# Tokens by place in a chunk of four, and S5 preparation moved from GpSimd to VectorE and ScalarE, in a two-layer S5 and attention kernel

## The chip, the cores and the metric

The kernel runs on one core of one Trainium2 chip. The metric is the device time of one execution in microseconds. A core has TensorE (PE in the profile, its weight loads PEld), VectorE (DVE), ScalarE (ACT), GpSimd (POOL) and SyncE (SP), which issues most of the transfers.

## The reference: what is computed

Two layers of half a feed-forward block, a mixer and another half block over 256 tokens of width 1024, all in float32. Cut to what matters here:

```python
for l in range(DEPTH):                       # 2
    x = x + 0.5 * swiglu(rms_norm(x, norm_ffn1[l]), ffn1_wi[l], ffn1_wo[l])
    h = rms_norm(x, norm_mix[l])
    (u, q_raw, k_cmp, v_cmp, k_sel, v_sel, k_win, v_win,
     nsa_gate, gate_a, gate_b) = jnp.split(h @ w_in[l], SPLIT_POINTS, axis=-1)
    y_a = s5_branch(u, ...)                  # 32 groups of 16 channels, 64 complex states each
    y_b = nsa_branch(q_raw, k_cmp, ...) @ nsa_w_up[l]
    merged = sigmoid(gate_a) * y_a + sigmoid(gate_b) * y_b
    x = x + merged @ w_out[l]
    x = x + 0.5 * swiglu(rms_norm(x, norm_ffn2[l]), ffn2_wi[l], ffn2_wo[l])
```

`s5_branch` discretizes a diagonal complex system (abar, bbar from lambda, dt, b), runs st[t] = abar st[t-1] + bbar u[t] over the tokens, and gives gelu(Re(c st) + d u), which goes through a gated product. `nsa_branch` rotates and normalizes q and k, compresses blocks of 32 tokens of k and v (stride 16) by a two-layer product, and attends to compressed, selected and windowed keys.

## The kernel before

**Products.** The wide products run as three passes of a split float32: `_split0` (L157 on ScalarE, L158 on VectorE) and `split` (L337, both engines) make a high part and a low part of each weight chunk of 128x1024, and `mm3` issues whi·hh, whi·hl and wlo·hh (L369 to L371). Chunks come through four buffers each of raw, high and low parts, and are asked for by `k.next()`, two ahead. A feed-forward block goes through 11 pieces of 256 hidden columns, whose results are transposed (L484) and split again.

**Background.** What isn't a wide product is written as generators that are pulled at every `k.next()` until their declared costs reach a budget. In ffn1 the generator is `prep`: `s5_scalars`, `s5_tables`, `s5_mats`. They build, from the layer's S5 parameters, the matrices G (input, `r` tiles), K (within a chunk of four tokens) and C (output) by complex products (`cmul`, L580 to L591: four products and two sums), by selections of a group's rows (L803), by transposes (L811) and by copies into place (L530 in `gcopy`). With `M=G` the four products of a `cmul` go to GpSimd (L580, L582, L587, L589) and the two sums to VectorE (L584, L591).

**The mixer.** `mix` takes h through chunks of w_in: 512 columns for u, 384 for compressed keys and values, 408 for the others, 512 for q, then the gates. After the first it makes uT (L1274, L1275: transposes and copies), and `s5_main` becomes the background: sixteen copies of 32 partitions (L868 on ScalarE, L870 on VectorE) turn uT into U4, which has the token within a chunk of four and the channel on the partitions and the chunk along the row; two sets of products G·U4 (L538, banks ya and yb); a rotation by tables (`rotate`, L925 to L933), two scans of 128x1024 (L885), a rotation back into Sp; the output products K·U4 and C·Sp (L903, tiles of 32 columns, 64 moving columns); gelu, and the split that gives yT. Meanwhile `compress` multiplies weights by strided columns of kc2 (L538, 45 moving columns), its result goes through `normrope` (L992 to L1005, on GpSimd L344, L345, L1004), is copied to kb (L1096), and is transposed in `compress2` (L1103). `normrope_q` does the same for q (L1056 to L1066).

**Order.** A scheduler in the framework orders the instructions of each engine at build time; each engine then runs its own list in order and waits for semaphores where it must. So an instruction that waits holds up all that stand behind it on its engine. The output leaves on SP's queue (L381).

Of the kernel before, what the change touches and what calls it, by code (L numbers as in the profile page):

```python
# [34 lines left out]

def shape_constants():
    a = np.zeros((128, 128 + CONST_W), np.float32)
    a[:, :128] = np.eye(128)
# [14 lines left out]
    put('cos', c.reshape(2, 128, 64).transpose(1, 0, 2))  # L53
    put('sin', s.reshape(2, 128, 64).transpose(1, 0, 2))
# [20 lines left out]
class Model:  # L75
# [497 lines left out]

    def cmul(k, o, a, b, tmp, cost, M=None, conj=False):

        V = k.nc.vector
        M = M or V
        c = cost if M is V else 0.0
        t0, t1 = tmp(), tmp()
        M.tensor_mul(t0, a[0], b[0])  # L580
        yield c
        M.tensor_mul(t1, a[1], b[1])  # L582
        yield c
# [3 lines left out]
        M.tensor_mul(t2, a[0], b[1])  # L587
        yield c
        M.tensor_mul(t3, a[1], b[0])  # L589
        yield c  # L590
# [130 lines left out]
    def s5_tables(k):  # L721
# [9 lines left out]
        k.gcopy(de, P['m4'][:, :, None].to_broadcast([128, 16, 64]))  # L731
# [37 lines left out]
    def s5_mats(k):  # L769
# [87 lines left out]
    def s5_main(k, uT):  # L857
# [35 lines left out]
        yt = r4().rearrange("p (a t s) -> p a t s", a=4, s=4)  # L893

        T = ((P['K'], U4), (P['C'][0], Sp[0]), (P['C'][1], Sp[1]))
        for h in range(2):
            bk = k.bank((128, 2, 4, 64), 'yb')
            for i, (m, v) in enumerate(T):
                for a in range(2):
                    for s in range(4):  # L900
                        for q in range(4):
                            p = h * 8 + a * 4 + q
                            nc.tensor.matmul(bk[q * 32:(q + 1) * 32, a, s], m[:, p, s * 32:(s + 1) * 32], v[:, p],  # L903
# [519 lines left out]
```

## Time and profile before

| | us |
|---|---|
| median of 3 runs | 1187.76 (1186.48 to 1188.71) |
| the profiled execution | 1188.25 |
| its span, first to last instruction | 1186.4 |
| PE busy | 1161.3 (98%) |
| DVE busy | 839.6 (71%) |
| ACT busy | 674.6 (57%) |
| POOL busy | 231.8 (20%) |

The span is 1.85 us shorter than the execution's time. Busy times of PE count overlapping matmuls once; a matmul of 512 columns is listed at 0.39 us, but the next starts 0.23 us later, and the distance between starts is what it costs in a run of them. On VectorE, too, an instruction starts some 0.08 us before the listed end of the one ahead of it. The two layers repeat: what stands at 225 us in the first stands at some 815 in the second.

### The profile page before, as it was taken

How to read it: one execution, taken by the hardware profiler on the slowest of the kernel's cores; microseconds unless marked ns; L12 is line 12 of the kernel's file. 1: busy time of each engine (PE TensorE's matmuls, PEld its weight loads, DVE VectorE, ACT ScalarE, POOL GpSimd, SP SyncE). 2: the span in 40 equal slices, each digit the busy share in tenths (PEclk: the TensorE clock that was granted, in tenths of full speed). 3: DMA queues.
4: the chain of work that ended last, by engine and by line, in shares of the span. 5: the costliest groups of instructions: out<-in, count | busy, mean ns of one | idle time of the engine just before them, and what ended most of it. 6: DMA issues, size and time to landing. Idle time of an engine off the chain costs nothing. (4 is left out here: it accounts for less than half of the span.)

```text
span 1186.4 us, 18796 instructions
## 1 busy us (share of the span) xinstructions
PE 1161.3 (98%) x6724; PEld 944.9 (80%) x6724; DVE 839.6 (71%) x1494; ACT 674.6 (57%) x1176; POOL 231.8 (20%) x285
## 2 busy tenths in 40 slices
PE   9999999999999999999999999999999999999998
PEld 6888777887877888888888887778778778888886
DVE  5797979586875755555667987886878756655554
ACT  6655554745765565554566555546657646655552
POOL 3002654044032000000030043711341310000000
PEclk9999999999999999999999999999999999999999
DMA  8766555364443566565565656445635435665662
GB/s 237 226 194 184 170 154 179 105 192 144 145 140 104 165 211 187 185 190 183 187 188 178 195 162 182 142 152 155 199 107 173 129 107 160 214 185 188 188 185 89
DMA packets 150078, 200.48 MB, mean 169 GB/s; under 512 B 9952, under 2 KB 120832, under 8 KB 149984
## 3 DMA queue, kind: packets, MB, share of 16 engines
q1 hardware_dynamic: 148848, 197.46, 54.3%
q0 software_dynamic: 1136, 1.82, 0.9%
q8 instruction: 53, 0.87, 0.3%
q14 instruction: 41, 0.34, 0.1%
HBM read 198.18 MB, written 1.05 MB: 168 GB/s over the span
## 5 line engine op out<-in xcount | busy, mean ns | idle before, releaser
L158 DVE SCALAR_TENSOR_TENSOR wlo<-raw,gcol,whi 128x512 fp32r<-128x512 f32 (+2 forms) x480 | 359.0, 785 | 110.0 <-ACT whi L157 107.6
L157 ACT ACTIVATE whi<-raw,gcol 128x512 fp32r<-128x512 f32 (+2 forms) x480 | 316.1, 710 | 193.0 <-PE gu L370 92.4
L369 PE MATMUL gu<-whi,hh 128*128 128x512 f32 (+2 forms) x944 | 372.2, 394 | 0.6 <-ACT whi L157 0.6
L371 PE MATMUL gu<-wlo,hh 128*128 128x512 f32 (+2 forms) x944 | 369.1, 396 | 2.3 <-DVE wlo L158 2.3
L370 PE MATMUL gu<-whi,hl 128*128 128x512 f32 (+2 forms) x944 | 368.9, 391 | 0.0
L337 DVE TENSOR_TENSOR wlo<-raw,whi 128x1024 fp32r<-128x1024 f32 x128 | 160.9, 1259 | 103.1 <-ACT whi L337 101.1
L337 ACT CAST whi<-raw 128x1024 fp32r<-128x1024 f32 x128 | 134.5, 1053 | 135.4 <-PE gu L370 112.1
L371 PEld LDWEIGHTS gu<-wlo,hh 128*128 128x128 f32 x944 | 177.8, 189 | 37.8 <-DVE wlo L158 2.6
L370 PEld LDWEIGHTS gu<-whi,hl 128*128 128x128 f32 x944 | 178.2, 189 | 35.2
L369 PEld LDWEIGHTS gu<-whi,hh 128*128 128x128 f32 x944 | 178.3, 189 | 34.5 <-ACT whi L157 0.8
L344 POOL TENSOR_SCALAR rs<-ss 128x1 f32<-128x1 f32 (+3 forms) x22 | 7.2, 328 | 378.4 <-ACT w2k L351 351.6
L370 PE MATMUL yb<-whi,w1k 128*128 128x512 f32 x176 | 71.4, 406 | 0.7 <-DVE w1k L337 0.7
L371 PE MATMUL yb<-wlo,w1k 128*128 128x512 f32 x176 | 69.2, 393 | 0.0
L369 PE MATMUL yb<-whi,w1k 128*128 128x512 f32 x176 | 69.0, 395 | 0.0
L370 PE MATMUL ya<-whi,w1k 128*128 128x512 f32 x176 | 68.8, 391 | 0.0
L371 PE MATMUL ya<-wlo,w1k 128*128 128x512 f32 x176 | 68.7, 391 | 0.0
L369 PE MATMUL ya<-whi,w1k 128*128 128x512 f32 x176 | 68.2, 393 | 0.0
L1207 POOL TENSOR_SCALAR w2k<-w2k,sm 128x128 f32<-128x128 f32 (+1 forms) x64 | 38.9, 629 | 100.6 <-ACT w2k L1191 63.2
L337 ACT CAST w1k<-tr 128x256 fp32r<-128x256 f32 x88 | 32.5, 370 | 45.7 <-PE tr L484 45.7
L501 DVE SCALAR_TENSOR_TENSOR w1k<-gu,rs,w1k 128x256 f32<-128x256 f32 x88 | 42.0, 479 | 16.2 <-ACT w1k L500 16.2
L500 ACT ACTIVATE w1k<-gu,rs 128x256 f32<-128x256 f32 x88 | 40.9, 467 | 20.0 <-PE gu L371 13.7
L337 DVE TENSOR_TENSOR w1k<-tr,w1k 128x256 fp32r<-128x256 f32 x88 | 36.7, 418 | 10.1 <-ACT w1k L337 10.0
(316 smaller groups left out, 1502.1 us busy)
## 6 DMA issues: line engine op xcount, KB each, us to landing
raw<-in_ffn_wi_dram SPq DMA_DIRECT2D x352, 256.0 KB, 3.3
raw<-in_ffn_wo_dram SPq DMA_DIRECT2D x88, 512.0 KB, 3.6
raw<-in_w_in_dram SPq DMA_DIRECT2D x48, 512.0 KB, 4.5
raw<-in_ssm_w_glu_dram SPq DMA_DIRECT2D x32, 256.0 KB, 3.4
raw<-in_w_out_dram SPq DMA_DIRECT2D x16, 512.0 KB, 3.3
raw<-in_cmp_w_dram SPq DMA_DIRECT2D x8, 512.0 KB, 4.8
raw<-in_nsa_w_up_dram SPq DMA_DIRECT2D x16, 256.0 KB, 4.1
raw<-in_w_in_dram SPq DMA_DIRECT2D x8, 408.0 KB, 4.2
```

Of the source, the lines that this page charges most:

```text
L157: k.hi_ins[i] = k.nc.scalar.activation(hi[:, s], r[:, s], AF.Copy, scale=c)
L158: k.lo_ins = k.nc.vector.scalar_tensor_tensor(lo[:, s], r[:, s], c, hi[:, s].bitcast(F32), op0=ALU.mult, op1=ALU.subtract)
L337: return k.nc.scalar.copy(hi, src), k.nc.vector.tensor_sub(lo, src, hi.bitcast(F32))
L344: k.nc.gpsimd.tensor_scalar(a, ss, scale, EPS, op0=ALU.mult, op1=ALU.add)
L369: mm(ps, a[0], b[0], start=first, stop=False)
L370: mm(ps, a[1], b[0], start=False, stop=False)
L371: return mm(ps, a[0], b[1], start=False, stop=last)
L500: m = nc.scalar.activation(sg, ps[t][:, :256], AF.Silu, scale=r[t])
L501: nc.vector.scalar_tensor_tensor(a, ps[t][:, 256:], r[t], sg, op0=ALU.mult, op1=ALU.mult)
L1207: G.tensor_scalar(w[:, i], p[:, i], cf[:, j:j + 1], 0.0, op0=ALU.mult, op1=ALU.add)
```

## The change

Tokens are stored by place: token t of each 128 goes to partition 32·(t mod 4) + t div 4 (`PLACE`; x is permuted before the launch, the constant tables alike, and `store` writes each 128x512 of the output by four transfers of 32 rows, alternately from SP's queue and ScalarE's). With that order, U4 is a 32x32-block transpose of u, done by VectorE straight behind the scaling by ScalarE, so the PE transposes, their copies and the sixteen narrow copies are left out. The output products swap their operands: U4 and Sp are stationary (64 columns), K and C move (128 columns), 48 matmuls a layer instead of 192; the result is put through gelu, transposed by PE (eight per layer) and split. kc2 is laid out so that the compression reads 33 adjacent columns instead of 45 strided ones.

In the S5 preparation, all products of `cmul` are on VectorE; the four selections (128x1024 each) are halved between ScalarE and VectorE, the ten copies into `ks` likewise, and the copy into `de` goes to ScalarE. The products of `normrope` and `normrope_q` move from GpSimd to VectorE. The budget per chunk grows from 0.75 to 1.2, and the generator waits longer before its first step.

```diff
+PLACE = 4 * (np.arange(128) % 32) + np.arange(128) // 32
...
+    def store(k, t, h, xs):
+        for u in range(4):
+            o = bass.AP(tensor=k.out.tensor, offset=k.out.offset + (t * 128 + u) * D + h * 512,
+                        ap=[[4 * D, 32], [1, 512]])
+            (k.nc.sync if u % 2 else k.nc.scalar).dma_start(o, xs[u * 32:(u + 1) * 32])
...
-                    k.nc.sync.dma_start(k.out[0, t * 128:(t + 1) * 128, h * 512:(h + 1) * 512], xs)
+                    k.store(t, h, xs)
...
-    def cmul(k, o, a, b, tmp, cost, M=None, conj=False):
+    def cmul(k, o, a, b, tmp, cost, conj=False):
...
-        M.tensor_mul(t0, a[0], b[0])
-        yield c
+        V.tensor_mul(t0, a[0], b[0])
+        yield cost
...
-                G.tensor_scalar(xx[:, :, g], X[i].rearrange("p a t c -> p (a t) c"), k.C('m64')[:, g:g + 1], 0.0,
-                                op0=ALU.mult, op1=ALU.add)
+                o, v, w = xx[:, :, g], X[i].rearrange("p a t c -> p (a t) c"), k.C('m64')[:, g:g + 1]
+                if g:
+                    V.tensor_scalar(o, v, w, None, op0=ALU.mult)
+                else:
+                    S.activation(o, v, AF.Copy, scale=w)
+                yield 1.2
...
-                k.gcopy(ks[t * 32:(t + 1) * 32, :, s], lag[r * 32:(r + 1) * 32])
+                (S.copy if (s + t) % 2 else V.tensor_copy)(ks[t * 32:(t + 1) * 32, :, s], lag[r * 32:(r + 1) * 32])
+                yield 0.3
...
-        U4 = r4().rearrange("p (a j) -> p a j", a=16)
-        for q in range(4):
-            for u in range(4):
-                o = U4[u * 32:(u + 1) * 32].rearrange("p (a q) j -> p q a j", q=4)[:, q]
-                i = uT[q * 32:(q + 1) * 32].rearrange("p a (j u) -> p u a j", u=4)[:, u]
-                if u % 2 == 0:
-                    S.copy(o, i)
-                else:
-                    V.tensor_copy(o, i)
...
-        T = ((P['K'], U4), (P['C'][0], Sp[0]), (P['C'][1], Sp[1]))
+        T = ((U4, P['K']), (Sp[0], P['C'][0]), (Sp[1], P['C'][1]))
         for h in range(2):
-            bk = k.bank((128, 2, 4, 64), 'yb')
...
-                            nc.tensor.matmul(bk[q * 32:(q + 1) * 32, a, s], m[:, p, s * 32:(s + 1) * 32], v[:, p],
...
+                        nc.tensor.matmul(bk[e * 64:(e + 1) * 64, q], v[:, p], m[:, p], start=(q == 0 and i == 0),
...
+            for s in range(4):
+                nc.tensor.transpose(bk[:, s], g[:, s].rearrange("p q c -> p (q c)"), k.id)
...
-            G.tensor_mul(T[ix + (a,)], Q[ix + (b,)], sg[ix + (a,)])
+            V.tensor_mul(T[ix + (a,)], Q[ix + (b,)], sg[ix + (a,)])
...
-            G.tensor_mul(t2[:, :, a], qn[:, :, b], sg[:, :, a])
+            V.tensor_mul(t2[:, :, a], qn[:, :, b], sg[:, :, a])
...
-                k.mm_cols(ps, [(w[:, m % 8], kc2[:, kv, :, m:m + 113:8])], m == 0, m == 15)
+                k.mm_cols(ps, [(w[:, m % 8], kc2[:, kv, m % 8, m // 8:m // 8 + 33])], m == 0, m == 15)
...
-            bk = k.bank((128, 4, 128))
-            for i in range(4):
-                nc.tensor.transpose(bk[:, i], u[:, i * 128:(i + 1) * 128], k.id)
-            S.copy(uT[:, :, t * 128:(t + 1) * 128], bk)
-        k.bg, k.budget = k.s5_main(uT), k.opt['B1']
+            V.transpose(U4[:, :, t * 32:(t + 1) * 32], u)
+        k.bg, k.budget = k.s5_main(U4), k.opt['B1']
...
-                for _ in range(4):
-                    yield 1.0
+                for _ in range(6):
+                    yield 1.1
...
-OPT = dict(nr=4, nh=4, LA=2, DLA=3, n1=10, n2=8, n4=7, n8=5, HP=2000, HN=2000, BG=0.75, FN=1, O1=22, WU=7, WV=7, SQ=1, LB=1, FB=2, O2=22, B1=1.0, B2=1.0)
+OPT = dict(nr=4, nh=4, LA=2, DLA=3, n1=10, n2=8, n4=7, n8=5, HP=2000, HN=2000, BG=1.2, FN=1, O1=22, WU=7, WV=7, SQ=1, LB=1, FB=2, O2=22, B1=1.0, B2=1.0)
```

The order of the instructions moves at three places that matter below. The names: wlo is the low part of a weight chunk, raw and whi its source and its high part, w1k and w2k are work tiles, s5q holds small S5 tables, r_n is a larger work tile.

VectorE late in the preparation, where the products for C begin; before, only their sums stand on VectorE:

```order
L584 TENSOR_TENSOR r_1691<-w2k 128x16x32
L158 SCALAR_TENSOR_TENSOR wlo<-raw,gcol,whi 128x512
L591 TENSOR_TENSOR r_1692<-w2k 128x16x32
L158 SCALAR_TENSOR_TENSOR wlo<-raw,gcol,whi 128x512 x3
L337 TENSOR_TENSOR w1k<-tr,w1k 128x256 x2
L337 TENSOR_TENSOR wlo<-raw,whi 128x1024 x2
```

and after:

```order
L590 TENSOR_TENSOR w2k<-s5q,w2k 128x512
L592 TENSOR_TENSOR w2k<-s5q,w2k 128x512
L597 TENSOR_TENSOR w2k<-s5q,w2k 128x512
L599 TENSOR_TENSOR w2k<-s5q,w2k 128x512
L349 TENSOR_TENSOR wlo<-raw,whi 128x1024
L860 COPY r_1535<-w2k 32x16x32 x2
L853 TENSOR_TENSOR w2k<-w2k 32x512
L349 TENSOR_TENSOR w1k<-tr,w1k 128x256
L594 TENSOR_TENSOR r_1614<-w2k 128x16x32
L601 TENSOR_TENSOR r_1615<-w2k 128x16x32
```

The four products and two of the copies into `ks` now stand on VectorE itself, ahead of and between the weight splits.

TensorE from the 384-column product on, where U4 is used first; before:

```order
L371 MATMUL gu<-wlo,hh 128x384
L538 MATMUL ya<-r_2347,r_1385 64x64 x2
L538 MATMUL ya<-r_2347,r_1484 64x64 x2
L538 MATMUL yb<-r_2347,r_1385 64x64
...
L371 MATMUL gu<-wlo,hh 128x408
L538 MATMUL yb<-r_2347,r_1484 64x64 x15
L538 MATMUL ya<-kc_1853,raw 64x45 x64
L903 MATMUL yb<-r_2347,r_1679 32x64 x9
```

and after:

```order
L382 MATMUL gu<-whi,hl 128x384
L550 MATMUL ya<-r_2320,r_1263 64x64 x16
L550 MATMUL ya<-r_2320,r_1379 64x64 x16
L383 MATMUL gu<-wlo,hh 128x384
...
L383 MATMUL gu<-wlo,hh 128x408
L550 MATMUL yb<-r_2320,r_1379 64x64 x3
L381 MATMUL gu<-whi,hh 128x408
...
L550 MATMUL ya<-kc_1851,raw 64x33 x64
L907 MATMUL yb<-r_1535,r_2320 64x128 x2
L907 MATMUL yb<-r_1614,r_2786 64x128 x2
L907 MATMUL yb<-r_1535,r_2320 64x128
L907 MATMUL yb<-r_1615,r_2787 64x128 x2
```

The products on U4 stand inside the 384-column product and the first quarter of the 408-column one instead of behind the former and the latter; behind the compression come products that read K and U4 (r_1535, r_2320) and the scanned states (r_2786, r_2787).

VectorE from the sum of squares of the compressed key to its copy kb; before:

```order
L994 TENSOR_REDUCE ss_2781<-nr_2779 32x1
L1056 TENSOR_REDUCE ss_2911<-w2k 128x8
L997 TENSOR_TENSOR nr_2786<-tr,rs 32x64
L999 TENSOR_TENSOR nr_2788<-nr_2786,cc 32x64
L158 SCALAR_TENSOR_TENSOR wlo<-raw,gcol,whi 128x512 x2
L1059 TENSOR_TENSOR w2k<-w2k,rs 128x512
L1005 TENSOR_TENSOR kc<-nr_2788,nr_2789 32x64
L158 SCALAR_TENSOR_TENSOR wlo<-raw,gcol,whi 128x512 x2
L1061 TENSOR_TENSOR w2k<-w2k,cg 128x512
L1096 COPY kb<-kc 32x128
```

and after:

```order
L1004 TENSOR_REDUCE ss_2759<-nr_2757 32x1
L1066 TENSOR_REDUCE ss_2896<-w2k 128x8
L1007 TENSOR_TENSOR nr_2764<-tr,rs 32x64
L1009 TENSOR_TENSOR nr_2766<-nr_2764,cc 32x64
L1014 TENSOR_TENSOR nr_2767<-nr_2764,cc 32x32 x2
L1015 TENSOR_TENSOR kc<-nr_2766,nr_2767 32x64
L170 SCALAR_TENSOR_TENSOR wlo<-raw,gcol,whi 128x512
L1106 COPY kb<-kc 32x128
```

The two narrow products stand on VectorE right behind the first one, and kb has one split ahead of it instead of four splits and two instructions on q.

## Rows read from the trace of the kernel before

**Rows 1.** The page's first part: busy time, share of the span and instructions.

```profile
PE 1161.3 (98%) x6724; PEld 944.9 (80%) x6724; DVE 839.6 (71%) x1494; ACT 674.6 (57%) x1176; POOL 231.8 (20%) x285
```

**Rows 2.** TensorE's waits: instruction, releaser, us in total, times, longest us.

```profile
PE ya L538 <- ACT r L868: 3.3, 2, 1.6
PE tr L1103 <- DVE kb L1096: 3.2, 2, 1.6
PE tr L811 <- DVE w1k L337: 2.9, 2, 1.4
PE tr L484 <- DVE w1k L501: 2.8, 2, 1.4
PE gu L371 <- DVE wlo L158: 2.3, 2, 1.4
...
PE tr L1287 <- ACT w1k L1282: 1.0, 2, 0.5
...
PE yb L370 <- DVE w1k L337: 0.7, 2, 0.3
```

**Rows 3.** Stretches: length, PE, PEld, DVE, ACT, POOL busy, granted clock, DMA.

```profile
120.00:130.00 10.00, 9.22 (x45) 7.22 (x43) 10.00 (x11) 5.63 (x10) 9.59 (x10) 1.00 0.46 122
...
180.00:190.00 10.00, 8.55 (x40) 6.72 (x40) 10.00 (x10) 4.48 (x7) 10.00 (x7) 1.00 0.31 105
...
280.00:290.00 10.00, 8.39 (x31) 6.49 (x30) 8.71 (x15) 6.93 (x12) 8.13 (x5) 0.83 0.54 150
```

**Rows 4.** Instructions of line 584, a sum of two products: min/median/max ns.

```profile
L584 DVE TENSOR_TENSOR r<-w1k x8: 424/840/842, 104.8 to 706.7; 128x256 f32<-128x256 f32 x8
L584 DVE TENSOR_TENSOR r<-w2k x8: 679/1004/1524, 165.2 to 776.7; 128x512 f32<-128x512 f32 x8
```

**Rows 5.** Timeline of VectorE near 126 us: start, us, instruction.

```profile
125.67 3.02 DVE L158 SCALAR_TENSOR_TENSOR wlo<-raw,gcol,whi 128x512 fp32r<-128x512 f32 x2
```

**Rows 6.** Instructions of line 158, the split: min/median/max ns.

```profile
L158 DVE SCALAR_TENSOR_TENSOR wlo<-raw,gcol,whi x480: 608/747/1617, 7.4 to 1160.7; 128x512 fp32r<-128x512 f32 x148, 128x384 fp32r<-128x384 f32 x6, 128x408 fp32r<-128x408 f32 x6
```

**Rows 7.** Instructions of line 870, the narrow copies on VectorE.

```profile
L870 DVE COPY r<-r x16: 377/381/388, 227.1 to 816.1; 32x256 f32<-32x256 f32 x16
```

**Rows 8.** Two longer stretches, columns as in rows 3.

```profile
145.00:175.00 30.00, 29.67 (x200) 23.93 (x199) 21.02 (x26) 14.85 (x24) 13.52 (x13) 1.00 0.52 157
...
257.00:284.00 27.00, 27.00 (x220) 19.32 (x218) 21.25 (x42) 16.82 (x32) 11.79 (x13) 1.00 0.56 163
```

**Rows 9.** Timeline of TensorE at 130 us; in brackets the wait and its releaser.

```profile
130.65 0.63 PE L811 MATMUL tr<-id,r 128*128 128x128 f32 x4 [1.42 <-DVE w1k L337]
131.03 0.47 PE L370 MATMUL gu<-whi,hl 128*128 128x512 f32 x1
```

**Rows 10.** Timeline of TensorE from 233 to 257 us.

```profile
233.57 1.39 PE L538 MATMUL ya<-r,r 128*64 128x64 f32 x40 [1.63 <-ACT r L868]
...
247.06 5.60 PE L538 MATMUL ya<-kc,raw 128*64 128x45 f32 x127
...
254.21 0.98 PE L903 MATMUL yb<-r,r 128*32 128x64 f32 x52
256.62 0.50 PE L371 MATMUL gu<-wlo,hh 128*128 128x512 f32 x1 [1.44 <-DVE wlo L158]
```

**Rows 11.** Timeline of VectorE near 253 us: the second scan.

```profile
253.65 2.28 DVE L885 TENSOR_TENSOR_SCAN r<-r,r 128x1024 f32<-128x1024 f32 x1
```

**Rows 12.** Timeline of TensorE near 371 us, in the attention.

```profile
371.65 1.96 PE L1228 MATMUL yb<-w2k,V 128*64 128x128 f32 x30
```

**Rows 13.** Timelines of VectorE, GpSimd and TensorE around kb.

```profile
279.78 0.21 DVE L999 TENSOR_TENSOR nr<-nr,cc 32x64 f32<-32x64 f32 x1
...
281.49 1.22 POOL L1004 TENSOR_TENSOR nr<-nr,cc 32x32 f32<-32x32 f32 x2
...
285.70 0.22 PE L1103 MATMUL tr<-id,kb 32*128 32x32 f32 x1 [1.61 <-DVE kb L1096]
...
286.43 0.63 PE L370 MATMUL gu<-whi,hl 128*128 128x512 f32 x1
286.86 0.63 PE L371 MATMUL gu<-wlo,hh 128*128 128x512 f32 x1
```

More of the change, by code (lines that the diff above doesn't have):

```diff
@@ L52, in shape_constants @@
     c, s = cs(np.arange(SEQ))
-    put('cos', c.reshape(2, 128, 64).transpose(1, 0, 2))
-    put('sin', s.reshape(2, 128, 64).transpose(1, 0, 2))
+    put('cos', c.reshape(2, 128, 64)[:, tok].transpose(1, 0, 2))
+    put('sin', s.reshape(2, 128, 64)[:, tok].transpose(1, 0, 2))
     n = np.arange(16)
@@ L572, in s5_load @@
         k.P = P
-    def cmul(k, o, a, b, tmp, cost, M=None, conj=False):
+    def cmul(k, o, a, b, tmp, cost, conj=False):
         V = k.nc.vector
-        M = M or V
-        c = cost if M is V else 0.0
         t0, t1 = tmp(), tmp()
-        M.tensor_mul(t0, a[0], b[0])
-        yield c
-        M.tensor_mul(t1, a[1], b[1])
-        yield c
+        V.tensor_mul(t0, a[0], b[0])
+        yield cost
+        V.tensor_mul(t1, a[1], b[1])
+        yield cost
         (V.tensor_add if conj else V.tensor_sub)(o[0], t0, t1)
@@ L586, in cmul @@
         t2, t3 = tmp(), tmp()
[L587 to L590, printed above, removed]
+        V.tensor_mul(t2, a[0], b[1])
+        yield cost
+        V.tensor_mul(t3, a[1], b[0])
+        yield cost
         (V.tensor_sub if conj else V.tensor_add)(o[1], t2, t3)
@@ L730, in s5_tables @@
         G.memset(sn[:, :, 0:1], 0.0)
-        k.gcopy(de, P['m4'][:, :, None].to_broadcast([128, 16, 64]))
+        k.nc.scalar.copy(de, P['m4'][:, :, None].to_broadcast([128, 16, 64]))
         G.memset(de[:, :, 0:1], 0.0)
@@ L781, in s5_mats @@
         for m in (1, 2, 3):
-            yield from k.cmul((X[0][:, :, 3 - m], X[1][:, :, 3 - m]), (bc(pw[m][0]), bc(pw[m][1])), bb, tmp1, 0.34, G)
+            yield from k.cmul((X[0][:, :, 3 - m], X[1][:, :, 3 - m]), (bc(pw[m][0]), bc(pw[m][1])), bb, tmp1, 0.34)
         CT = []
@@ L892, in s5_main @@
             yield from k.rotate(Sp, Z, P['cs'], P['sn'], slice(h * 8, h * 8 + 8), -1)
[L893 to L895 removed]
+        yh, yl = r4(F32R), r4(F32R)
+        T = ((U4, P['K']), (Sp[0], P['C'][0]), (Sp[1], P['C'][1]))
         for h in range(2):
[L897 to L910 removed]
+            bk = k.bank((128, 4, 128), 'yb')
+            for q in range(4):
+                for i, (v, m) in enumerate(T):
+                    for e in range(2):
+                        p = (2 * h + e) * 4 + q
+                        nc.tensor.matmul(bk[e * 64:(e + 1) * 64, q], v[:, p], m[:, p], start=(q == 0 and i == 0),
+                                         stop=(i == 2), skip_group_check=True)
+                yield 0.6
+            g = k.sb([128, 4, 4, 32], "w2k", k.opt['n2'])
+            S.activation(g.rearrange("p s q c -> p q s c"), bk.rearrange("p q (s c) -> p q s c", s=4),
+                         AF.Gelu_apprx_tanh)
+            yield 0.6
+            bk = k.bank((128, 4, 128))
+            for s in range(4):
+                nc.tensor.transpose(bk[:, s], g[:, s].rearrange("p q c -> p (q c)"), k.id)
+            o = [y.rearrange("p (a s j) -> p s a j", a=8, s=4)[:, :, 4 * h:4 * h + 4] for y in (yh, yl)]
+            k.split(bk.rearrange("p s (a j) -> p s a j", a=4), *o)
+            yield 0.8
         k.yT = [t.rearrange("p (a t) -> p a t", a=4) for t in (yh, yl)]
[L912 removed]
     def rotate(k, out, x, cs, sn, sl, sign):
@@ L977, in nsa_prep @@
         N['cg'], N['sg'], N['cc'] = cg, sg, cc
-        kc2 = k.sb([128, 2, 3, 128], "kc2", 1)
-        nc.gpsimd.memset(kc2[:, :, 2], 0.0)
+        kc2 = k.sb([128, 2, 8, 34], "kc2", 1)
         bk = k.bank((128, 32))
         nc.tensor.transpose(bk, N['pe'], k.id[:32, :32])
-        V.tensor_copy(kc2[:, :, 2, 0:16], bk.rearrange("p (a b) -> p a b", a=2))
+        for kv in range(2):
+            V.tensor_copy(kc2[:, kv, :, 32:34], bk[:, kv * 16:(kv + 1) * 16].rearrange("p (i m) -> p m i", i=2))
         N['kc2'] = kc2
@@ L1287, in mix @@
                 nc.tensor.transpose(bk[:, i], u[:, i * 128:(i + 1) * 128], k.id)
-            S.copy(kvT[:, :, t * 128:(t + 1) * 128], bk)
+            for i in range(2):
+                S.copy(kvT[:, i, t * 128:(t + 1) * 128].rearrange("p (j u) -> p u j", u=4),
+                       bk[:, i].rearrange("p (u j) -> p u j", u=4))
         N['gate'], N['o'] = [], []
@@ L1382, in prep @@
                         k.late_setup()
-                for _ in range(4):
-                    yield 1.0
+                for _ in range(6):
+                    yield 1.1
                 yield from k.s5_scalars()
```

36 lines of the change are left out of this document (15 added, 21 removed).

## The prediction, made before the changed kernel was run

> **What bounds the kernel now.** I read the busy shares first: TensorE is busy for 1161.3 of 1186.4 us [rows 1], and every other engine has room on average. So time can come from two places only: from the 25 us in which TensorE does nothing, and from TensorE's own work. The list of TensorE's waits comes next [rows 2]: every entry counts two, one for each layer. In order of time they are: three waits while the S5 matrices are prepared inside ffn1 (L811, yb L370, L484, all on w1k from VectorE), one for the copies that rearrange u (L538 on ACT L868, with L1287 behind it), one for a weight split that comes late (L371 on wlo), one before the transpose of kb (L1103). The stretches tell what the engines do around them [rows 3]: at 120 to 130 and 180 to 190 VectorE is busy for all 10.00 us, with GpSimd at 9.59 and 10.00; at 280 to 290 the granted clock is 0.83.
>
> VectorE is full there because GpSimd works beside it. The same 128x256 sum takes 424 ns at best and 840 at the median, and the 128x512 one 679 to 1524 [rows 4]; two splits take 3.02 us while GpSimd multiplies [rows 5], 1.51 each, where the median split is 747 ns [rows 6]. I read this as one resource that both engines need. The Trainium skill, SBUF — State Buffer, section "Who interferes with whom", says that a VectorE instruction with two SBUF inputs contends with a GpSimd instruction that reads SBUF, and that one of them is blocked until the other is done. The trace agrees so far as 840 against 424 can show it.
>
> **S5 preparation.** The change takes 28 products per layer (12 of 128x256, 16 of 128x512), four selections of 128x1024 and ten copies of 32x512 off GpSimd. VectorE gets all products, half the selections and six of the copies. At the best durations of [rows 4], less some 0.08 by which neighbours overlap, the products add 12 x 0.34 + 16 x 0.60 = 13.7 us. A selection and a wide copy have no row on VectorE; the nearest are the sum of half the width, 0.68, and the copy of 32x256, 0.38 [rows 7]. I take 1.0 and 0.6 (bounds 0.7 and 1.4, 0.4 and 0.8), since neither reads two tiles: 2.0 + 3.6, so 19 us added per layer. What falls away is the excess: four sums of either size on L584 per layer, 0.42 and 0.33 too long, as many on L591, which I take alike (6 us), and of the splits roughly four in each of the two full stretches, 0.75 too long [rows 5, 6], 6 us. VectorE's net load grows by some 7 us per layer, while it had 9.0 us without work between 145 and 175 alone [rows 8]. The waits that came from slowed splits and sums, 2.9 + 2.8 + 0.7 [rows 2], should therefore go: −6.4. But the budget of 1.2 instead of 0.75 draws the same work within five eighths of the weight chunks. I allow 0.7 per layer for a new wait late in preparation (bounds 0 and 3.2): +1.4. Together **−5.0**, bounds −6.4 and 0.
>
> **From u to the first late split (225 to 257 us; the same near 815 to 845).** U4 is made by sixteen narrow copies, and TensorE waits for them from 231.9 until 233.57 [rows 10], and 0.5 for L1287 [rows 2]. The change puts one scaling on ScalarE and one 128x512 transpose on VectorE per half. No row has such a transpose; the nearest, a sum of that size, is 0.68 us [rows 4]. Even at twice that, U4 is there well before the first L550, which now stands behind 29 of the 48 matmuls of the 384-column product. So 2.1 us a layer of wait go. What is late next? VectorE's chain: products on yb, two scans, products on the scans, and only then the next wlo. Before, yb was finished at 247.0, ahead of the compression, and TensorE got its wlo at 256.62 [rows 10]. After, the last products on U4 stand in front of 36 of the 48 matmuls of 408 columns. The 384-column product itself ended near 230.6 and would end at 229.8 without eight transposes (below); from there I count 128 passes on U4 (4.0), five departures from full width (1.25), four transposes (0.4) and 12 matmuls of 0.23 x 408/512 = 0.18 (2.2): yb is finished near 237.6. Then VectorE runs 5 + 9 products and sums of 0.60, two scans of 2.3 [rows 11], some 1.0 of small instructions and a split of 0.72: 14.7 us, so wlo is ready at 252.3. TensorE meanwhile has 36 x 0.185 = 6.7 us of the 408-column product, the compression, and then L907. The compression is 127 passes of 45 strided columns in 5.60 us, 44 ns each [rows 10]; 33 adjacent columns cost at most that, and at least 33/64 of a pass of 64 adjacent ones (40 in 1.39 us, 30 ns when the 0.2 of the last is taken off [rows 10]), 16 ns: 2.0 to 5.6 us. TensorE is thus at L907 between 246.3 and 249.9, and waits for the first scanned state (250.0) and its partner (250.7) in all of that range. What the compression gains is swallowed here. With 2.9 us of work behind that wait the matmul that stood at 256.62 starts at 253.6: 3.0 earlier per layer, **−6.0** in all. Bounds: −8.4 (wlo's 252.3 alone decides) and −3.6 (the U4 wait gone and little else). On the compression alone the Trainium skill, SBUF — State Buffer, section "Door 1: The DMA port swizzle", states that an access which crosses to a new line of 16 bytes pays, as each of a stride of eight fp32 does. By it the pass falls to the lower of the two prices, 16 ns, and the sum stays as it is, since VectorE's chain ends last.
>
> **S5 output (257 to 284).** TensorE is busy for all 27.00 us [rows 8], so its work counts. Of L903's 384 passes per layer 314 remain there, at 15 ns (52 in 0.98 us less the 0.22 of one [rows 10]); they become 62 passes of L907, whose nearest row is L1228, also 64 stationary and 128 moving columns: 30 in 1.96 us, some 63 ns [rows 12]. 4.7 against 3.9. The first full-width matmul after a departure is listed at 0.50 [rows 10] where 0.39 is usual; I take as much before the departure, 0.25 in all, an estimate. About twelve departures become four: −2.0. Eight transposes of y are new: 0.38 a set of four [rows 9], +0.8. That is −2.0; splits come close behind their use there, so I take two thirds, −1.4 per layer: **−2.8**, bounds 0 and −4.2.
>
> **The kb wait.** kb waits for L1005, which waits for two GpSimd products (281.49, 1.22 us [rows 13]) in GpSimd's queue; then two splits and L1061 stand before kb on VectorE. TensorE waits 1.61, and the next eight matmuls step at 0.43 us instead of 0.23 (286.43 to 286.86 [rows 13]) with the clock at 0.83 over those 10 us [rows 3]. The change puts these products on VectorE directly behind L999, which ends at 280.0, with one split before kb: 3 x 0.2 + 0.7 + 0.2, so kb is there near 281.5, while TensorE came to its transpose at 284.1. Gone: 1.6 + 8 x 0.2 = 3.2 per layer, **−6.4**, bounds −6.4 and 0. The products L1064 on q go to VectorE too, 4 x 0.34 a layer; the splits beside them, slowed now, pay for that.
>
> **The end.** The output leaves as four transfers on two queues instead of one; no row shows such a quarter, so 0 with 0.5 to either side.
>
> **Sum.** −5.0 − 6.0 − 2.8 − 6.4 = −20.2 from the profiled 1188.25 gives 1168.05; that execution lies 0.5 above the median 1187.76, so I predict **1167.5** us.
>
> **Rivals.** *VectorE becomes the bound in preparation.* For it: VectorE is at 10.00 of 10 in two stretches already [rows 3], and 19 us more are drawn faster. Against it: GpSimd's share of that load falls out. If the first part's gain is lost and a wait of the present size stays, the sum is −15.2: 1172.5; with 1.6 us of slow clock behind one such wait per layer, 1176. *Slower.* The same place, but the moved products keep the slow price although GpSimd is silent, because their broadcast operands made them slow: 12 x 0.84 + 16 x 1.0 = 26 us per layer where I have 13.7. With the lead used up, all 12.4 us stand in TensorE's way, and −15.2 + 24.8 gives 1197. It decides from 7.6 us per layer on, where the other gains are eaten. Against it: 424 and 679 stand in the same group of instructions. *The wait before L907 costs the clock, or kb's wait only shifts.* In my own count TensorE waits 0.8 to 4.4 us before L907; if the clock falls behind it as behind L1103, or the kb term is lost, 3.2 to 6.4 us come back: 1171 to 1174. *Nothing swallowed.* If yb is finished earlier than I count and VectorE leads throughout, TensorE goes through L907 from 246.3: 250.2 instead of 253.6 per layer, 1161.
>
> **How the numbers follow.** My forecast (1163 to 1170) 0.50; VectorE bound in preparation 0.16; wait before L907 or kb kept 0.14; nothing swallowed 0.11; slower 0.07; the waits exchanged for others of equal size, 1187, 0.02. The range 1159 to 1179 leaves out the slower case, the exchanged waits and the far ends of the others. About 0.2% (2.4 us) is what a measurement of this kernel can tell from no change. Faster by more 0.88, within it 0.05 (the exchanged waits, and cases near the point at which the slower one decides), slower 0.07.
>
> **What would show it.** Right: VectorE's 128x256 products at 0.42 and splits at 0.75 throughout; no TensorE wait for w1k from VectorE, none for U4, none before the transpose of kb, and clock 1.00 there; a wait of 0.8 to 4.4 us at L907 or at the first wlo behind it. Wrong: GpSimd silent and VectorE's products still at 0.84 and above; or a wait for wlo or w1k near 165 to 190 us; or a clock below 1.00 behind L907.

## The result, and the profile after

The changed kernel takes 1166.39 us in the median of four executions (1165.54 to 1167.36), the kernel before 1187.6 beside it; the ratio is 0.9822 (95% interval 0.9807 to 0.9837). The profiled execution took 1167.36, with a span of 1165.6. The prediction was 1167.5, range 1159 to 1179.

The page's first part of after, beside [rows 1]: GpSimd falls from 231.8 to 96.0 us, and VectorE, which took over most of that, is busy for less time than before (827.1 instead of 839.6).

```profile
PE 1153.3 (99%) x6148; PEld 939.7 (81%) x6148; DVE 827.1 (71%) x1578; ACT 671.9 (58%) x1176; POOL 96.0 (8%) x177
```

TensorE's waits of after, complete, beside [rows 2] (instruction, releaser, us in total, times, longest):

```profile
PE yb L907 <- DVE r L936: 3.1, 2, 1.5
PE gu L381 <- ACT r L1322: 1.8, 2, 1.3
PE ya L300 <- POOL w1k L294: 1.4, 1, 1.4
PE gu L448 <- ACT hh L349: 0.7, 1, 0.7
```

All entries of [rows 2] are gone. Two are new: before the S5 output, for the scanned state (predicted), and before a gate product, for a tanh on ScalarE (not predicted). The other two stand in the kernel before as well (there L288 and L436, 1.7 and 0.7). The stretches that answer to [rows 3], and the one between 145 and 175 of [rows 8]:

```profile
120.00:130.00 10.00, 10.00 (x53) 8.27 (x52) 5.12 (x8) 6.57 (x13) 2.12 (x4) 1.00 0.79 222
...
180.00:190.00 10.00, 10.00 (x48) 8.19 (x47) 8.85 (x16) 4.44 (x7) 0.00 (x0) 1.00 0.72 226
...
145.00:175.00 30.00, 29.91 (x137) 24.27 (x137) 29.75 (x56) 18.63 (x29) 0.00 (x0) 1.00 0.48 140
...
280.00:290.00 10.00, 10.00 (x48) 8.21 (x47) 7.87 (x16) 5.38 (x10) 1.85 (x2) 1.00 0.59 171
```

TensorE is full where it had gaps, and the clock is 1.00 at 280 to 290. VectorE has no room left between 145 and 175: 29.75 of 30 us, and yet TensorE loses 0.09 there. The instructions that answer to [rows 4] and [rows 6] show why that is enough (min/median/max ns):

```profile
L594 DVE TENSOR_TENSOR r<-w1k x8: 406/414/418, 79.7 to 683.4; 128x256 f32<-128x256 f32 x8
L594 DVE TENSOR_TENSOR r<-w2k x8: 679/682/687, 155.2 to 757.7; 128x512 f32<-128x512 f32 x8
...
L170 DVE SCALAR_TENSOR_TENSOR wlo<-raw,gcol,whi x480: 608/746/754, 7.1 to 1139.9; 128x512 fp32r<-128x512 f32 x148, 128x384 fp32r<-128x384 f32 x6, 128x408 fp32r<-128x408 f32 x6
```

The sum of 128x256 took 424 to 842 ns, now 406 to 418; the longest split fell from 1617 to 754.

Where the time went can be read by pairing the weight matmuls of both traces by their number: both run 4416 of them, in the same order but for passes that change places with near neighbours (in the last stage of the table the pair is a whi·hl pass before and a whi·hh pass after, 0.2 us apart in a run of them). Starts in us:

| stage, by the matmul that ends it | before | after | gained, layer 1 + layer 2 | predicted |
|---|---|---|---|---|
| ffn1 with the S5 preparation | 211.76; 797.98 | 208.06; 786.08 | 3.69 + 3.41 = 7.1 | 5.0 |
| u to the first late split | 256.62; 842.84 | 251.85; 829.08 | 1.08 + 1.87 = 3.0 | 6.0 |
| S5 output | 278.30; 864.54 | 271.28; 848.07 | 2.26 + 2.72 = 5.0 | 2.8 |
| the kb wait | 296.46; 882.71 | 287.68; 863.05 | 1.75 + 3.18 = 4.9 | 6.4 |
| all the rest | | | −0.30 + 1.11 = 0.8 | 0 |
| sum | | | 20.8 | 20.2 |

So the sum is right while its terms are off by up to 3 us, and the errors cancel. Three of the four terms lie outside the bounds that I gave them (7.1 against at most 6.4, 3.0 against at least 3.6, 5.0 against at most 4.2): that the total came within 1.1 us is in part luck.

### The profile page after: what moved, and what is told of

Read it like the earlier page. It is cut to its first block, busy times and chain, and to the rows that moved or that the text cites. A ratio compares the mean times of both kernels' runs of the same rounds, so it can differ in the third digit from the quotient of the medians.

```text
span 1165.6 us, 17595 instructions
## 1 busy us (share of the span) xinstructions
PE 1153.3 (99%) x6148; PEld 939.7 (81%) x6148; DVE 827.1 (71%) x1578; ACT 671.9 (58%) x1176; POOL 96.0 (8%) x177
## 4 chain that ended last, share of the span: by engine, by line
PE 95%; DVE 3%; ACT 1%; issue 0%; POOL 0%; DVEq 0%; ACTq 0%; POOLq 0%
PE gu L381 20%; PE gu L383 20%; PE gu L382 20%; PE yb L382 4%; PE yb L383 4%; PE yb L381 4%; PE ya L383 4%; PE ya L381 4%; PE ya L382 4%; PE tr L496 2%; PE yb L1238 1%; PE yb L907 1%; PE tr L375 1%; PE tr L1227 1%; PE gu L448 1%; PE ya L1194 1%
## 5 line engine op out<-in xcount | busy, mean ns | idle before, releaser
L170 DVE SCALAR_TENSOR_TENSOR wlo<-raw,gcol,whi 128x512 fp32r<-128x512 f32 (+2 forms) x480 | 335.6, 738 | 108.2 <-ACT whi L169 106.2
L381 PE MATMUL gu<-whi,hh 128*128 128x512 f32 (+2 forms) x944 | 373.5, 396 | 1.8 <-ACT r L1322 1.8
L382 PE MATMUL gu<-whi,hl 128*128 128x512 f32 (+2 forms) x944 | 367.6, 389 | 0.0
L349 DVE TENSOR_TENSOR wlo<-raw,whi 128x1024 fp32r<-128x1024 f32 x128 | 156.5, 1225 | 120.0 <-ACT whi L349 117.2
L381 PEld LDWEIGHTS gu<-whi,hh 128*128 128x128 f32 x944 | 177.9, 188 | 36.3 <-ACT r L1322 2.6
L382 PEld LDWEIGHTS gu<-whi,hl 128*128 128x128 f32 x944 | 178.1, 189 | 34.8 <-issue 0.2
L382 PE MATMUL yb<-whi,w1k 128*128 128x512 f32 x176 | 71.2, 406 | 0.2
L382 PE MATMUL ya<-whi,w1k 128*128 128x512 f32 x176 | 68.7, 392 | 0.0
L381 PE MATMUL yb<-whi,w1k 128*128 128x512 f32 x176 | 68.0, 393 | 0.0
L381 PE MATMUL ya<-whi,w1k 128*128 128x512 f32 x176 | 67.6, 394 | 0.0
L1217 POOL TENSOR_SCALAR w2k<-w2k,sm 128x128 f32<-128x128 f32 (+1 forms) x64 | 35.1, 568 | 103.8 <-DVE sm L1209 48.6
```

The source lines that it names most:

```text
L170: k.lo_ins = k.nc.vector.scalar_tensor_tensor(lo[:, s], r[:, s], c, hi[:, s].bitcast(F32), op0=ALU.mult, op1=ALU.subtract)
L349: return k.nc.scalar.copy(hi, src), k.nc.vector.tensor_sub(lo, src, hi.bitcast(F32))
L381: mm(ps, a[0], b[0], start=first, stop=False)
L382: mm(ps, a[1], b[0], start=False, stop=False)
L1217: G.tensor_scalar(w[:, i], p[:, i], cf[:, j:j + 1], 0.0, op0=ALU.mult, op1=ALU.add)
```

## The experiments

All edits are to the changed kernel unless said otherwise; times are medians, with the median of the kernel before on the same chip in brackets. The changed kernel itself took 1166.39 on one chip and 1167.63 on another, so a difference to it from another chip holds to about 1 us. No run takes back the order of the tokens or the swapped output products alone; what these gave is read from the traces, by stages.

**Preparation back on GpSimd.**

```diff
-            yield from k.cmul((X[0][:, :, 3 - m], X[1][:, :, 3 - m]), (bc(pw[m][0]), bc(pw[m][1])), bb, tmp1, 0.34)
+            yield from k.cmul((X[0][:, :, 3 - m], X[1][:, :, 3 - m]), (bc(pw[m][0]), bc(pw[m][1])), bb, tmp1, 0.34, G)
...
-                (S.copy if (s + t) % 2 else V.tensor_copy)(ks[t * 32:(t + 1) * 32, :, s], lag[r * 32:(r + 1) * 32])
-                yield 0.3
+                k.gcopy(ks[t * 32:(t + 1) * 32, :, s], lag[r * 32:(r + 1) * 32])
...
-BG=1.2
+BG=0.75
```

(`cmul`, the products for C, the selections, the copy into `de` and the delays likewise as in the kernel before).

> The changed kernel with the S5 preparation as it was: products, selections and copies on GpSimd, budget 0.75, the old delays. In the trace of the changed kernel the matmul that ends ffn1's background comes 4.3 us earlier in layer 1 and 3.7 in layer 2. Theory (the preparation's term is that large, and what follows only shifts): 1166.4 + 8.0 = 1174.4, with the three waits on w1k back at 1.4, 0.3 and 1.4 us per layer. Rival (the predicted term of 5.0, the rest of the 8.0 being other parts of the change): 1171.4. Rival (what follows is paced by VectorE, so that part of it comes back): 1169 or less.

1171.37 (1187.13), 5.0 more than the changed kernel. The three waits are back, and VectorE's sum of 128x256 is at 840 again in the median:

```profile
PE tr L823 <- DVE w1k L349: 2.8, 2, 1.4
PE tr L496 <- DVE w1k L513: 2.6, 2, 1.3
...
PE yb L382 <- DVE w1k L349: 0.7, 2, 0.3
...
L596 DVE TENSOR_TENSOR r<-w1k x8: 424/840/842, 104.4 to 698.4; 128x256 f32<-128x256 f32 x8
```

In its trace the end of ffn1 is no earlier than before in layer 1 (211.73 against 211.76). Beside the changed kernel's trace some 6.9 us are given up in the two preparations, and 2.7 of them are left at the last weight matmul: 3.5 come back in layer 1 behind the preparation, 0.7 in layer 2. Two things that differ account for part of it. The wait for the tanh (1.8 at L1322, which is L1319 in this run's kernel) isn't among its waits, and the clock fell behind the wait for the scanned state in layer 1 alone, where it fell in both layers of the changed kernel's trace. So 1171.37 is the number of the first rival, but not by its mechanism: the term is larger than 5.0, and part of it comes back, as the second rival had it. (Between the two profiled executions it is 3.1, the changed kernel's slowest of four against this run's fastest.)

**The preparation's move alone**, on the kernel before:

```diff
-            yield from k.cmul((X[0][:, :, 3 - m], X[1][:, :, 3 - m]), (bc(pw[m][0]), bc(pw[m][1])), bb, tmp1, 0.34, G)
+            yield from k.cmul((X[0][:, :, 3 - m], X[1][:, :, 3 - m]), (bc(pw[m][0]), bc(pw[m][1])), bb, tmp1, 0.34)
...
-BG=0.75
+BG=1.2
```

(and the other lines of the same list, the other way round).

> The kernel before with only the preparation moved to VectorE and ScalarE, budget 1.2 and the longer delays. Theory: 8.0 us less than before, 1179.7; the waits on w1k gone, VectorE's 128x256 products at 0.42 us; the waits for U4, wlo and kb as before (1.6, 1.4 and 1.6 us). Rival (the predicted term): 1182.8. Rival (VectorE, now fuller, delays what follows): over 1184.

1180.01 (1187.13): 7.1 less, as the stage shows, and it is still there at the end. The waits of the mixer stay, two as they were and the one for wlo a little longer (2.8, where it was 2.3):

```profile
PE ya L538 <- ACT r L871: 3.3, 2, 1.6
PE tr L1106 <- DVE kb L1099: 3.2, 2, 1.6
PE gu L371 <- DVE wlo L158: 2.8, 2, 1.5
```

The clock fell behind the wait for kb in layer 1 (1.61 us), and not behind that in layer 2 (1.62), where its mean from 864 to 874 us is 1.00; in the trace of the kernel before it fell behind both.

**The pace.** Three runs change one number, the budget per chunk; the first has the old delays before the preparation as well.

```diff
-BG=1.2
+BG=0.75
```

```diff
-BG=1.2
+BG=1.0
```

```diff
-BG=1.2
+BG=1.6
```

> The changed kernel with the preparation's budget of 0.75 per chunk and the old delays, its work still on VectorE and ScalarE. Theory (the engine decides, not the pace; VectorE had room): 1165.5 to 1167.5, no wait on w1k of over 0.3 us. Rival (the faster draw is needed, since at 0.75 the preparation runs into the end of ffn1): 1168 to 1172 and a wait near the end of ffn1. Rival (1.2 draws too fast and the slower pace takes away the small wait that is left at 161.7 us): 1165.5 or below.

> The changed kernel with a budget of 1.0 per chunk. At 0.75 the products stood behind the last weight split of ffn1 and TensorE waited for them; the declared costs grow by 21.5 per layer with this change (12 x 0.34, 16 x 0.6, 4 x 1.2, 10 x 0.3, all 0 before), so the budget has to grow with them. Theory: at 1.0 the preparation ends near 190 us, before ffn1 does: 1165 to 1168. Rival (a rest is still left when ffn1 ends): 1170 to 1185 with a wait for ya or x near 207 us.

> The changed kernel with a budget of 1.6 instead of 1.2 per chunk. VectorE is busy for 29.75 of 30 us between 145 and 175 in the changed kernel. Theory (the prediction's first rival: drawn faster, VectorE becomes the bound in the preparation): the same work in three quarters of the chunks, about 4 us per layer more than VectorE can take beside the splits, of which its lead hides a part: waits on w1k or wlo again, 1168 to 1174. Rival (the lead covers it): 1165 to 1167.

| budget | 0.75 | 1.0 | 1.2 | 1.6 |
|---|---|---|---|---|
| us | 1194.82 | 1170.66 | 1166.39 | 1195.63 |

Both ends are slower than the kernel before, with the engines as in the changed kernel. At 0.75 the preparation isn't done when ffn1 ends, and the rest of it stands on VectorE in front of what TensorE needs next (a wait of TensorE from its timeline, and the stretch around it):

```profile
207.45 0.79 PE L382 MATMUL ya<-whi,w1k 128*128 128x512 f32 x1 [4.63 <-DVE w1k L349]
...
200.00:210.00 10.00, 3.79 (x10) 2.50 (x11) 10.00 (x17) 0.37 (x1) 0.00 (x0) 0.56 0.46 131
```

At 1.0 a rest of the same wait is left (1.7 us at most for w1k at L382). At 1.6 VectorE holds TensorE up inside the preparation, as the first rival had it, already where the small tables are computed; waits for ScalarE's parts of the transposed results (5.1 us, `yb` and `ya` at L381) are among its waits too, and I did not follow these:

```profile
PE tr L496 <- DVE w1k L513: 7.0, 3, 3.0
PE tr L496 <- DVE w2k L756: 4.3, 1, 4.3
...
60.00:70.00 10.00, 9.85 (x38) 8.03 (x39) 9.68 (x60) 2.24 (x4) 0.00 (x0) 0.83 0.26 74
...
130.00:140.00 10.00, 8.01 (x31) 6.17 (x30) 9.82 (x18) 5.94 (x12) 0.00 (x0) 0.83 0.30 101
```

I had expected no cost at 0.75, none at 1.0 and at most 8 us at 1.6. All three expectations failed, the first and the last by more than 20 us.

**Key and query products back on GpSimd.**

```diff
-            V.tensor_mul(T[ix + (a,)], Q[ix + (b,)], sg[ix + (a,)])
+            G.tensor_mul(T[ix + (a,)], Q[ix + (b,)], sg[ix + (a,)])
-            V.tensor_mul(t2[:, :, a], qn[:, :, b], sg[:, :, a])
+            G.tensor_mul(t2[:, :, a], qn[:, :, b], sg[:, :, a])
```

> The changed kernel with the narrow products of the key and query normalization (lines 1014 and 1074) back on GpSimd. Theory (the kb wait came from these two products in GpSimd's queue): TensorE waits for kb again, 1 to 1.6 us per layer, and the clock falls behind it, 1.6 more: 1169 to 1172, layer 1 less than layer 2 because a wait for ScalarE's L1322 of 1.3 us stands there already. Rival (it came from GpSimd being loaded and slowed by the rest): kb is in time, 1166 to 1168.

1171.90 (1187.13), 5.5 more. The kb wait is back, longer than before, and GpSimd's timeline shows the same queue although the preparation has left it: rs takes 1.65, then the two narrow products 1.23.

```profile
PE tr L1113 <- DVE kb L1106: 5.2, 2, 3.1
...
273.04 1.65 POOL L357 TENSOR_TENSOR rs<-rs,mh 128x8 f32<-128x8 f32 x1
274.65 1.23 POOL L1014 TENSOR_TENSOR nr<-nr,cc 32x32 f32<-32x32 f32 x2
```

So the queue was the cause, not the load by the preparation. The clock fell behind the kb wait in layer 2 (3.08 us) and not behind that in layer 1 (2.08); before L907 it fell in layer 1 (1.55) and not in layer 2 (1.54).

**The compression's columns.** One run reads 45 adjacent columns, one 33 at a stride of eight.

```diff
-                k.mm_cols(ps, [(w[:, m % 8], kc2[:, kv, m % 8, m // 8:m // 8 + 33])], m == 0, m == 15)
+                k.mm_cols(ps, [(w[:, m % 8], kc2[:, kv, m % 8, m // 8:m // 8 + 45])], m == 0, m == 15)
```

```diff
-        kc2 = k.sb([128, 2, 8, 34], "kc2", 1)
+        kc2 = k.sb([128, 2, 34, 8], "kc2", 1).rearrange("p k c m -> p k m c")
```

> The changed kernel with the compression reading 45 adjacent columns instead of 33 (the 12 more are zeros that nothing uses). Before, a pass of 45 strided columns cost 44 ns; now one of 33 adjacent columns costs 30.6. Theory (the stride cost, and below it the load of 64 stationary columns is the floor): still 30 to 31 ns, 128 passes in 3.9 us. Rival (the number of columns): 42 to 44 ns, 5.5 us. The whole time hardly moves either way, since TensorE waits behind it for the scanned state.

> The changed kernel with the compression reading 33 columns at a stride of eight numbers. Theory (each strided column costs 0.98 ns and 30 ns is the floor): 32 to 33 ns a pass, 4.2 us for 128. Rival (the stride is free, the number of columns decided): 30.6 ns, 3.9 us. Rival (stride costs a fixed sum): 44 ns, 5.6 us.

TensorE's timeline of the changed kernel, of the one with 45 adjacent and of the one with 33 strided columns:

```profile
240.91 3.92 PE L550 MATMUL ya<-kc,raw 128*64 128x33 f32 x128
```

```profile
240.92 3.94 PE L550 MATMUL ya<-kc,raw 128*64 128x45 f32 x128
```

```profile
241.28 4.24 PE L550 MATMUL ya<-kc,raw 128*64 128x33 f32 x128
```

Listed time over passes: 33 and 45 adjacent columns cost the same, some 30 ns a pass; 33 strided ones 33, and 45 strided ones (three runs of 15 at that stride) 44 [rows 10]. So between 33 and 45 a strided column costs about 1 ns, and no pass here costs less than 30. Of the 14 ns that the change gained, the order in memory alone would have given all, and the smaller number of columns alone 11: either was nearly enough. Times 1168.22 and 1165.46 in one execution each (1187.19) say no more than that nothing large hangs on it. With 33 strided columns the compression ends later and the wait before L907 is shorter in both layers (here the first):

```profile
247.00 1.40 PE L907 MATMUL yb<-r,r 128*64 128x128 f32 x12 [1.25 <-DVE r L936]
```

The clock stayed at 1.00 behind both.

**K products first.** In the changed kernel TensorE waits for the scanned state behind only four passes that don't need it. The edit puts all products of a half that need U4 and K alone in front (and declares three costs of 0.8 for four of 0.6); a second one does so for both halves.

```diff
-            for q in range(4):
-                for i, (v, m) in enumerate(T):
+            for i, (v, m) in enumerate(T):
+                for q in range(4):
```

> The changed kernel with the S5 output products of a half in another order: all eight that need only U4 and K first, then those with the scanned states. In the changed kernel TensorE waits 1.54 us for the scanned state in each layer, and the next matmuls step at 0.43 instead of 0.23. Theory (the wait costs itself and the clock): with 16 passes and four wide matmuls ahead, 2.2 us, the state is there; TensorE then waits about 1.0 for wlo; the clock stays at 1.00; about 2.3 us per layer earlier, 1162. Rival (VectorE's chain paces it all the same and the clock falls behind the wait for wlo): 1165 to 1167. Rival (what is won here is lost to the later wait for ScalarE's L1322): 1163 to 1165.

> As the run before it, and the products with K of the second half also ahead of those with the scanned states. Theory: TensorE has 1.0 us more that needs no state, so nothing waits for a state; wlo at about 249.3 us is what it waits for, 1.1 us, as in the run before it: 1162, the same within 1 us. Rival (the wait for wlo is long enough to lower the clock where it stands alone): 1165 to 1166.

> The changed kernel once more, beside the next run. In its first profile the clock fell behind the wait at L907 in both layers and that execution took 1167.36; its other executions took 1165.54 to 1166.44. Theory (whether the clock falls there varies from execution to execution, 1.6 us each): times between 1164 and 1167.4, and a profile in which zero or one of the two places has matmul steps of 0.43 us is faster by 1.6 for each that has none. Rival (the clock falls there always, the spread is something else): both places at 0.43 again.

> The changed kernel with the K products of a half first, once more, for its distance to the changed kernel on the same chip. Theory: 1164.4, 1 to 2 us less than the changed kernel, since the wait for the state of 1.5 us per layer goes, its clock with it, and 0.8 for a weight's high part and 0.3 for its low part come in its place. Rival: no distance (under 0.5 us).

1164.53 (1187.19) the first time, where three executions took 1164.41 to 1164.60 and one 1168.79; 1164.55 (1164.37 to 1164.71) the second, beside 1167.63 (1166.81 to 1167.71) for the changed kernel on the same chip. I had expected 1162. The wait for the state is gone in both layers, and smaller ones stand in its place, the tanh of L1322 in both layers now (waits of the second run, and TensorE's timeline):

```profile
PE gu L381 <- ACT r L1322: 2.6, 2, 1.3
PE gu L381 <- ACT whi L169: 1.8, 2, 1.0
...
PE gu L383 <- DVE wlo L170: 0.3, 1, 0.3
...
246.78 0.50 PE L381 MATMUL gu<-whi,hh 128*128 128x512 f32 x1 [0.80 <-ACT whi L169]
247.12 0.40 PE L382 MATMUL gu<-whi,hl 128*128 128x512 f32 x1
```

This version beats both kernels: ratio 0.9808 (0.9795 to 0.9821) against 0.9833 (0.9819 to 0.9846) for the changed one, both to the kernel before. With both halves in front it is 1165.76, in two groups, 1164.13 and 1164.41, 1167.12 and 1167.56; in the profile, of an execution of the second group, TensorE waits 2.4 us for a weight's high part in layer 2 and the clock falls behind it, which I did not follow further.

The clock is told apart by two runs that wait for the same state. With the changed kernel's first profile and the run with 45 columns TensorE starts again at 246.63, after 1.54 us in both (changed kernel first, then 45 columns):

```profile
246.63 1.70 PE L907 MATMUL yb<-r,r 128*64 128x128 f32 x12 [1.54 <-DVE r L936]
248.26 0.80 PE L381 MATMUL gu<-whi,hh 128*128 128x512 f32 x1
...
249.28 0.63 PE L381 MATMUL gu<-whi,hh 128*128 128x512 f32 x1
249.70 0.63 PE L382 MATMUL gu<-whi,hl 128*128 128x512 f32 x1
250.26 1.66 PE L907 MATMUL yb<-r,r 128*64 128x128 f32 x18
251.85 0.51 PE L383 MATMUL gu<-wlo,hh 128*128 128x512 f32 x1
```

```profile
246.63 1.40 PE L907 MATMUL yb<-r,r 128*64 128x128 f32 x12 [1.54 <-DVE r L936]
247.96 0.50 PE L381 MATMUL gu<-whi,hh 128*128 128x512 f32 x1
...
250.32 0.50 PE L383 MATMUL gu<-wlo,hh 128*128 128x512 f32 x1
```

The same matmul starts at 251.85 and at 250.32; the granted clock from 245 to 255 is 0.83 and 1.00, and while it is down wide matmuls follow each other by 0.42 us (249.28 to 249.70) instead of 0.23, the lower of the clock's two levels, 1.2 GHz instead of 2.4:

```profile
245.00:255.00 10.00, 8.32 (x52) 5.91 (x52) 9.74 (x23) 8.29 (x14) 2.77 (x4) 0.83 0.79 255
```

```profile
245.00:255.00 10.00, 8.33 (x62) 6.14 (x61) 9.74 (x24) 8.28 (x14) 2.69 (x4) 1.00 0.80 261
```

So the lower clock costs 1.5 us at this place. In layer 2, from the start on the scanned state to the matmul that answers to 842.84 of the kernel before, it costs 1.2 to 1.4: 4.43 and 4.62 us in the two profiles of the changed kernel, 3.26 with 33 strided columns, where the clock held. The second profile of the changed kernel has it in both layers again. Over its eight timed executions the mean granted clock goes with the time: 0.997 at 1167.36 to 1167.71, 0.999 at 1166.35 to 1166.81, 1.000 at 1165.54. That looks like two, one and no such place, but only executions with two of them have a trace, and the steps are nearer to 1 us than to 1.5, so this reading stays open. That the fall isn't certain is shown: TensorE waited 1.54 or 1.55 us before the products on the scanned state at fifteen places in eight traces, and the clock fell behind nine of them.

## Why the prediction was right, point by point

**S5 preparation: right mechanism, 5.0 predicted, 7.1 measured, above the bound of 6.4.** Two errors. The waits were priced by their listed idle time, 6.4. But that time begins at the listed end of the matmul ahead, 0.39 after its start, while the next could have started 0.23 after it; each wait is 0.16 us longer than listed. At 130.65 [rows 9] the matmul ahead starts at 128.84, so 1.81 − 0.23 = 1.58 are lost and not 1.42; the three waits of layer 1 come to 3.69 so, which is what the stage gained. And the new wait of 0.7 per layer, which I allowed because the larger budget "draws the same work within five eighths of the weight chunks", did not come: 0.09 us is left. That step was wrong. The change also gives declared costs to work that had none: 12 x 0.34 + 16 x 0.6 + 4 x 1.2 + 10 x 0.3 = 21.5 per layer. In the traces the first sum of 128x256 and the first of 128x512 lie 60.4 us apart before (104.8 and 165.2 [rows 4]) and 75.5 after (79.7 and 155.2): the pace fell. The budget had to grow with the costs, and the run at 0.75 shows the price of leaving it, 28 us.

**The load on VectorE.** The moved products take 0.41 and 0.68 as I priced them; the selection of 1024 columns takes 0.75 where I took 1.0, the copy of 32x512 0.42 where I took 0.6, both inside their bounds. The slower rival falls with that: broadcast operands are not what made the products slow.

**U4 and the first late split: 6.0 predicted, 3.0 measured, below the bound of 3.6.** The chain is as I counted it. It starts 3.7 us earlier, since ffn1 ends earlier; with that taken off I had the first state at 246.3 and the matmul of 256.62 at 249.9. TensorE started on that state at 246.63, after a wait of 1.54. The term failed at its last step, the work from the first state to that matmul, 3.6 in my count (0.7 to the partner, then "2.9 us of work behind that wait"): it took 5.2 at the lower clock, and 3.7 in the run where the clock held. I had that as a rival (the wait before L907 costs the clock), 0.14 with the kb case, at 1.6 per layer, and a clock below 1.00 there as a sign of being wrong; the two traces show 1.5 in layer 1. It came true in the profiled execution, and the surplus of other terms paid for it. That the compression's gain is swallowed was right; of my prices of 16 to 44 ns a pass it measured 30, which is what I had read for 64 adjacent columns in the same row.

The Trainium skill, SBUF — State Buffer, section "Door 1: The DMA port swizzle", on columns in lines of 16 bytes: 45 adjacent columns at 30 ns a pass against 45 strided ones at 44 agree with it, and so do 33 at 30 against 33, if by little. The fall to 16 ns that I took with it does not come: something else holds a pass of 64 stationary columns at 30 here, and no run shows what.

**S5 output: 2.8 predicted, 5.0 measured, above the bound of 4.2.** I had counted 2.0 per layer and taken two thirds because splits might come late. They did not: 2.26 in layer 1, where a new wait of 0.55 is taken off already, and 2.72 in layer 2. The discount had no row behind it. The count was wrong as well, and its errors nearly cancel. I placed 314 of L903's passes in this stretch; 122 are there, and 192 run as one block later. After, 22 of L907's passes are there in layer 1 (28 in layer 2) and 40 in a later block, and the eight transposes of y stand outside too (the stretch with L903 alone, and TensorE's timelines before and after):

```profile
257.00:284.00 27.00, 4.31 (x122) 2.69 (x122) 1.00 0.56 163
```

```profile
309.29 2.89 PE L903 MATMUL yb<-r,r 128*32 128x64 f32 x192
```

```profile
300.25 2.40 PE L907 MATMUL yb<-r,r 128*64 128x128 f32 x40
```

At 15 ns before and 60 ns after (2.40 for 40) the passes of this stretch gain some 0.1 to 0.5 us a layer. The departures from full width were ten and became four, not twelve and four; so the rest, 2.3 to 2.6 a layer, comes to about 0.4 us each where I took 0.25. That price is an estimate, and no run tests it alone.

**The kb wait: 6.4 predicted, 4.9 measured.** Layer 2 gained 3.18 of 3.2. In layer 1 TensorE waits for ScalarE's L1322 in the place of kb (ScalarE's timeline, then TensorE's):

```profile
272.75 5.50 ACT L169 ACTIVATE whi<-raw,gcol 128x512 fp32r<-128x512 f32 x8 [1.43 <-PE gu L382]
278.16 0.67 ACT L1322 ACTIVATE r<-gu,rh 128x512 f32<-128x512 f32 x1
...
278.88 0.50 PE L381 MATMUL gu<-whi,hh 128*128 128x512 f32 x1 [1.27 <-ACT r L1322]
```

The tanh that frees the bank stands behind eight high parts on ScalarE. Before, it started at 285.18, and TensorE stood still for kb until 285.70, so this wait was hidden. The clock's share of the term, 1.6 per layer, was no certainty either: with the preparation's move alone the clock held behind the kb wait in layer 2. I asked for each removed stall what is late next on VectorE, and not on ScalarE.

**The end** cost nothing either way: from the start of the last weight matmul to the end of the span 4.7 us in both traces.

## What to carry to other kernels

When work moves between engines under a scheduler that spends a budget of declared costs, sum the declared costs before and after; the budget that fits can be narrow (here 1.2, with 0.75 and 1.6 both slower than the kernel that was to be improved). Price a wait from start to start, not by the listed idle time, and when a stall goes, ask on every engine what finishes next. A right total can hide terms that are off by half, so check the total by stages.

## What the runs showed of the hardware

- TensorE's clock fell behind nine of fifteen waits of 1.54 or 1.55 us before the products on the scanned state and held behind six, at the same place too (0.83 and 1.00 over 245 to 255); it held behind both waits of 1.25 us. Behind waits of 2.08 and 3.08 us in one run it fell only at the longer. I cannot say from these runs what decides it.
- A pass of a float32 matmul with 64 stationary columns costs some 30 ns with 33, 45 or 64 [rows 10] adjacent moving columns, 33 with 33 at a stride of eight, 44 with 45 at that stride.
- GpSimd's operation on rs of 128x8 (L357, L345 in the kernel before) takes 1.64 to 1.65 us at all twelve places of three traces (before, changed, products back on GpSimd), with nothing on VectorE beside it (877.51 us before) as with splits there; so that duration is its own here. It took longer, 2.01, at two places with the preparation back on GpSimd, beside three splits on VectorE.
